# Seven block products for pairs of gate tiles, and output tables made later, in a hybrid attention/SSM block

## The chip, the cores and the metric

The kernel runs on one core of one Trainium2 chip. The metric is the device time of one execution in microseconds (us); a smaller number is better. TensorE (PE) does the matrix products, VectorE (DVE) and ScalarE (ACT) the elementwise work, GpSimd (POOL) a little of it; SyncE (SP) and ACT issue most transfers (DMAs).

## The reference, cut to what matters

```python
h = rms_norm(x)                                   # x: 1024 tokens x 1024
q, k, v, z_a, u, z_s, g_a, g_s = split(h @ W_in)  # 512 wide each, g_a and g_s 1024
y_a = band_attention(q, k, v) * silu(z_a) @ W_attn_out
y_s = GLU(gelu(S5(u))) * silu(z_s) @ W_ssm_out
x = x + (sigmoid(g_a + bias) * y_a + sigmoid(g_s + bias) * y_s) @ W_out
out = rms_norm(x)
```

All in float32. The kernel splits each float32 operand in a high and a low part of the type fp32r, and takes three products: high·high, high·low, low·high.

## The kernel before

`h^T` lies in four tiles: `hT[0]` holds the high parts, `hT[1]` the low parts, each in two tiles `q` = 0, 1 of [128, 4, 1024] (4 of the 8 row tiles of h^T, all 1024 tokens). A *projection* (`proj_task`, with `proj` and `mm3`) takes one 128-row tile of W_in^T, whose raw form `w_raw` is loaded by SP and split into `w_hi` (ACT) and `w_lo` (DVE), and makes two halves of 512 tokens; a half is 8 × 3 = 24 matmuls of 128x512 into one PSUM bank, and an eviction.

The order in time: normalisation and V; projections with the SSM scan beside them; attention, woven into further projections; then, from about 463 us on, the part that the change concerns:

1. The last three g_a tiles (`ga[NGA:]`) and eight g_s tiles (`gs_task`). A g_s eviction is a sigmoid on ACT into a tile `sg`, which SP stores to `sgs_dr` in DRAM.
2. The K=512 stages, through `o_task`: attention output `a_all` (8 tasks), GLU `glu` (8), SSM output `so_all` (8). A task loads a weight tile `o_raw`, splits it (`o_hi`, `o_lo`) and makes two halves of 12 matmuls in three PSUM banks `mm`; between halves it gives way (a "step" of the loops below, numbered n). The moving operands are split before: `split_tiles(za)` for attention output, `split_y_ssm` for GLU, `split_tiles(zs)` for SSM output. `merged` is the sum of both gated branches, kept in `mgd`.
3. W_out. The product of `merged` with W_out is made for pairs of token tiles with seven block products instead of eight (the Winograd form of Strassen's scheme): products P1 to P7 of a left block (A11, A12, A22, S1 to S4) with a right block (B11, B21, B22, T1 to T4), named in `MATES`; `ORDER` names the three banks a, b, c that they add up in. A block product is 4 × 3 = 12 matmuls. `operand` splits a left block.

The right blocks of W_out are 28 *tables* (seven names × four row tiles), each a high and a low part. `make_tables` makes them: for each of four row pairs j it loads two `wo_raw` tiles (in the two slots of `rows`), forms T1 to T4 with four DVE operations, and splits seven results (seven ACT and seven DVE operations). In the kernel before, it runs during the g_s tiles, one step for three k-steps of the projections, through the two slots of `qk_pools[1]` that the last g_a tiles leave; each of the 28 goes to DRAM (`wt_dr`, SP) and comes back by `load_table` (ACT's queue) in the K=512 stages, into the places listed in `SPOTS`.

Memory is given out in pools: a pool has a number of slots for each tag, and a new tile waits until a slot is free. `vp` has eight slots of 4 KB a partition: they hold V during attention, then the high and low parts of the four y tiles of attention output, then those of SSM output. Which instruction comes next on an engine is decided before the run by a planner: it takes, in a simulated time, the ready instruction that the program names first; `tc.high_priority()` puts some ahead, `tc.issue_after` some behind. On the chip each engine then goes through its list in order.

Of the kernel before, what the change touches and what calls it, by code (L numbers as in the profile page):

```python
# [9 lines left out]
F32 = mybir.dt.float32  # L10
F32R = mybir.dt.float32r
# [15 lines left out]
T8 = 8  # L27
# [17 lines left out]
def trunk_kernel(ctx: ExitStack, tc: tile.TileContext, x, x_t, ng, w_m, w_v, bias, a_re, a_im, log_dt,  # L45
# [53 lines left out]
    def split_hi(hi, src):  # L99
        act.activation(out=hi, in_=src, func=AF.Copy)  # L100
# [1010 lines left out]
    def o_task(src, y, evac, before=None, late=False):  # L1111
# [21 lines left out]
        return (o_dma(src), o_split, run, 2)  # L1133

    def gs_task(m):
        def evac(half, ps):
            sg = half_tile()
            act.activation(out=sg, in_=ps, func=AF.Sigmoid, bias=gb[:, KT + m:KT + m + 1])
            nc.sync.dma_start(out=sgs_dr[m][:, cut(half)], in_=sg)
        return proj_task(w_m[28 + m], evac)  # L1140

# [58 lines left out]

    hs, ls = split_tiles(za, vp, "v", "y")
    ya[0].extend(hs)
    ya[1].extend(ls)
    ygr = []

    def load_y(b):
        yr = rows.tile([P, T8, NJ], F32, tag="yr", name="yr")
        nc.sync.dma_start(out=yr, in_=y_dr[b].rearrange("t p j -> p t j"))
        ygr.append(yr)

    wt_dr = {(name, j): dr.tile([P, 2, HALF], F32, name=f"wt_{name}_{j}")
             for name in ("B11", "B21", "B22", "T1", "T2", "T3", "T4") for j in range(4)}

    def make_tables():

        for j in range(4):
# [8 lines left out]
            def keep(name, src):  # L1228
                t = qk_pools[1].tile([P, 2, HALF], F32R, tag="blk", name="wt")
                split_hi(t[:, 0, :], src)  # L1230
                split_lo(t[:, 1, :], src, t[:, 0, :])
                nc.sync.dma_start(out=wt_dr[name, j], in_=t.bitcast(F32))

            def sum_tile():
                return rest.tile([P, HALF], F32, tag="t", name="t", bufs=1)

# [18 lines left out]
    tables = make_tables()  # L1255
    gen = stream.run(ga[NGA:] + [gs_task(m) for m in range(KT)], a_all[:2])
    for _ in range(4 * KT):
        with tc.issue_after(last_turn[0]):
            next(gen)
    for n, _ in enumerate(gen):  # L1260
        if n % 3 == 2:
            next(tables, None)
        if n in (3 * 36 + 4, 3 * 36 + 12):
            load_y((n - 112) // 8)
    wp_cm.__exit__(None, None, None)
    h16_cm.__exit__(None, None, None)
    wo_cm = tc.tile_pool(name="wo", reuse_waits="tile", side="right", bufs=14)
    wo = wo_cm.__enter__()
    mgd.extend(wo.tile([P, 4, L], F32, tag=f"mgd{q}", name="mgd", bufs=1) for q in range(2))

    def split_y_ssm(b):
        v3 = "c (j t) -> c j t"
        src = ygr[b].rearrange("c t j -> c j t")
        hi = wo.tile([P, L], F32R, tag="wb", name="g_hi")
        lo = wo.tile([P, L], F32R, tag="wb", name="g_lo")
        split_hi(hi.rearrange(v3, t=T8), src)
        split_lo(lo.rearrange(v3, t=T8), src, hi.rearrange(v3, t=T8))
        yg[0].append(hi)
# [35 lines left out]

    def operand(src, pool_, tag):
        t = pool_.tile([P, 2, 4, P], F32R, tag=tag, name="a")
        split_hi(t[:, 0], src)
        split_lo(t[:, 1], src, t[:, 0])
        return t

    for n, _ in enumerate(stream.run(so_all)):
        if n > 1 and len(wb) < 28:
            load_table()
        if n == 2 * KT - 2:
            fin_op["A11"] = operand(block(0, "A11"), rows, "yr")
            s3 = rest.tile([P, HALF], F32, tag="t", name="s3", bufs=1).rearrange("p (k m) -> p k m", m=P)
            tt(s3, block(0, "A11"), block(0, "A21"), SUB)
            fin_op["S3"] = operand(s3, rows, "yr")
    assert len(wb) == 28
    rest_cm.__exit__(None, None, None)  # L1330

    ORDER = [("P1", "a", (0,)), ("P2", "b", (0,)), ("P6", "a", (1,)), ("P5", "c", (3,)), ("P7", "a", (3,)),
             ("P3", "c", (1,)), ("P4", "a", (2,))]

# [5 lines left out]
    nc.scalar.dma_start(out=fg_b, in_=fg.partition_broadcast(P))  # L1346
    banks = [(ps_m, "mm")] * 3 + [(ps_2, "s")] * 2 + [(ps_t, "pt")] * 2
    taken = [0]

    def bank():  # L1350
        p_, tag = banks[taken[0] % 7]
        taken[0] += 1
        return p_.tile([P, HALF], F32, tag=tag, name="c")

    for n in range(KT // 2):
# [49 lines left out]
        for pn, bk, to in order:  # L1405
# [13 lines left out]
            for cs in cuts:  # L1419
                for k in range(4):  # L1420
                    w = wb[bn, k]
                    o, h, l = pss[bk][:, cs], w[:, 0, cs], w[:, 1, cs]
                    pe.matmul(o, a[:, 0, k, :], h, start=new and k == 0, stop=False, skip_group_check=True)  # L1423
                    pe.matmul(o, a[:, 0, k, :], l, start=False, stop=False, skip_group_check=True)  # L1424
                    pe.matmul(o, a[:, 1, k, :], h, start=False, stop=k == 3, skip_group_check=True)  # L1425
# [84 lines left out]
```

## Time and profile before

| | us |
|---|---|
| median of 3 runs (lowest, highest) | 800.01 (799.62, 802.39) |
| the profiled execution | 801.95 |
| its span, first to last instruction | 800.2 |
| mean granted clock of TensorE | 0.994 |

The profile is of one execution. A group line reads: source line, engine, operation, output tile <- input tiles, shape, count | busy us, mean ns of one | idle time of the engine before them and who ended it. A line of a tile reads: line, engine, operation, names, count: shortest/median/longest ns, first and last start in us. A line of waits reads: who <- whom: total us, times, longest us.

### The profile page before, as it was taken

How to read it: one execution, taken by the hardware profiler on the slowest of the kernel's cores; microseconds unless marked ns; L12 is line 12 of the kernel's file. 1: busy time of each engine (PE TensorE's matmuls, PEld its weight loads, DVE VectorE, ACT ScalarE, POOL GpSimd, SP SyncE). 2: the span in 40 equal slices, each digit the busy share in tenths (PEclk: the TensorE clock that was granted, in tenths of full speed). 3: DMA queues.
4: the chain of work that ended last, by engine and by line, in shares of the span. 5: the costliest groups of instructions: out<-in, count | busy, mean ns of one | idle time of the engine just before them, and what ended most of it. 6: DMA issues, size and time to landing. Idle time of an engine off the chain costs nothing.

```text
span 800.2 us, 11133 instructions
## 1 busy us (share of the span) xinstructions
PE 786.2 (98%) x3882; PEld 654.3 (82%) x3882; DVE 533.2 (67%) x1382; ACT 371.4 (46%) x670; POOL 115.6 (14%) x162
## 2 busy tenths in 40 slices
PE   8999999999999999999999999999999999999996
PEld 6778888888887888888888888888888888888885
DVE  6899987978746878887555443444163345777874
ACT  5552547546346566666454584434250132122543
POOL 4450021020202233333231100000000000000000
PEclk8999999999999999999999999999999999999999
DMA  8614342423430111110200154898866237722232
GB/s 317 237 28 131 109 91 93 123 57 122 119 138 28 44 44 43 43 43 5 67 27 27 45 196 164 318 331 300 311 212 252 93 106 260 265 65 107 106 117 94
DMA packets 45127, 105.58 MB, mean 132 GB/s; under 512 B 5968, under 2 KB 15184, under 8 KB 45072
## 3 DMA queue, kind: packets, MB, share of 16 engines
q1 hardware_dynamic: 36544, 84.42, 30.5%
q10 hardware_dynamic: 7376, 18.10, 6.6%
q0 software_dynamic: 1152, 2.36, 1.5%
q8 instruction: 30, 0.49, 0.3%
q14 instruction: 25, 0.20, 0.1%
HBM read 75.02 MB, written 29.85 MB: 131 GB/s over the span
## 4 chain that ended last, share of the span: by engine, by line
PE 89%; DVE 6%; ACT 1%; issue 1%; DMA 1%; POOL 0%; DVEq 0%; ACTq 0%
PE mm L108 22%; PE mm L106 22%; PE mm L107 22%; PE c L1423 3%; PE c L1424 3%; PE c L1425 3%; PE pt L957 2%; PE pv L976 2%; PE s L928 1%; PE pv L975 1%; DVE p L930 1%; PE s L929 1%; DVE tl L103 1%; PE pt L456 1%; PE b L482 1%
## 5 line engine op out<-in xcount | busy, mean ns | idle before, releaser
L106 PE MATMUL mm<-hT,w_hi 128*128 128x512 f32 x576 | 233.3, 405 | 0.0
L108 PE MATMUL mm<-hT,w_lo 128*128 128x512 f32 x576 | 226.0, 392 | 0.7 <-DVE w_lo L103 0.7
L107 PE MATMUL mm<-hT,w_hi 128*128 128x512 f32 x576 | 225.4, 391 | 0.0
L108 PEld LDWEIGHTS mm<-hT,w_lo 128*128 128x128 f32 x576 | 108.1, 188 | 24.7 <-DVE w_lo L103 1.1
L107 PEld LDWEIGHTS mm<-hT,w_hi 128*128 128x128 f32 x576 | 108.6, 189 | 16.5 <-issue 0.4
L106 PEld LDWEIGHTS mm<-hT,w_hi 128*128 128x128 f32 x576 | 108.4, 188 | 16.2 <-issue 0.2
L937 ACT ACTIVATE p<-p,mx 128x640 f32<-128x640 f32 (+2 forms) x64 | 44.4, 694 | 33.3 <-DVE mx L89 16.8
L103 DVE TENSOR_TENSOR tl<-pt,th 128x512 fp32r<-128x512 f32 (+2 forms) x72 | 43.0, 600 | 24.5 <-ACT th L100 23.9
L939 POOL TENSOR_SCALAR p<-p,sm 128x640 f32<-128x640 f32 (+2 forms) x64 | 42.5, 666 | 111.5 <-DVE sm L938 80.8
L100 ACT ACTIVATE th<-pt 128x512 fp32r<-128x512 f32 (+2 forms) x72 | 37.6, 523 | 44.6 <-PE pt L957 44.0
L100 ACT ACTIVATE w_hi<-w_raw 128x1024 fp32r<-128x1024 f32 x36 | 38.0, 1055 | 39.3 <-PE mm L107 28.7
L103 DVE TENSOR_TENSOR w_lo<-w_raw,w_hi 128x1024 fp32r<-128x1024 f32 x36 | 44.2, 1229 | 17.2 <-ACT w_hi L100 17.1
L930 DVE CUSTOM_DVE_ANT_0 p<-s,bias 128x320 f32<-128x320 f32 (+2 forms) x96 | 44.2, 485 | 17.2 <-PE s L929 16.7
L106 PE MATMUL mm<-y_hi,o_hi 128*128 128x512 f32 x128 | 49.9, 390 | 0.0
L107 PE MATMUL mm<-y_lo,o_hi 128*128 128x512 f32 x128 | 49.8, 389 | 0.0
L108 PE MATMUL mm<-y_hi,o_lo 128*128 128x512 f32 x128 | 49.8, 390 | 0.0
L100 ACT ACTIVATE o_hi<-o_raw 128x512 fp32r<-128x512 f32 x24 | 15.1, 632 | 70.1 <-PE mm L107 55.5
L1423 PE MATMUL c<-wb,a 128*128 128x512 f32 (+1 forms) x116 | 44.6, 385 | 0.5 <-DVE x L85 0.5
L1424 PE MATMUL c<-wb,a 128*128 128x512 f32 (+1 forms) x116 | 44.7, 385 | 0.0
L1425 PE MATMUL c<-wb,a 128*128 128x512 f32 (+1 forms) x116 | 44.2, 384 | 0.0
L957 PE MATMUL pt<-ident,p 128*128 128x128 f32 x240 | 38.1, 273 | 0.0
L976 PE MATMUL pv<-tl,vt 128*128 128x256 f32 x144 | 36.2, 281 | 1.0 <-DVE tl L103 1.0
(225 smaller groups left out, 1472.3 us busy)
## 6 DMA issues: line engine op xcount, KB each, us to landing
w_raw<-in_w_m_dram SPq DMA_DIRECT2D x36, 512.0 KB, 3.8
x<-in_x_dram SPq DMA_DIRECT2D x16, 512.0 KB, 7.5
wt_T<-wt SPq DMA_DIRECT2D x16, 512.0 KB, 3.4
wb<-wt_T ACTq DMA_DIRECT2D x16, 512.0 KB, 4.9
wt_B<-wt SPq DMA_DIRECT2D x12, 512.0 KB, 4.3
wb<-wt_B ACTq DMA_DIRECT2D x12, 512.0 KB, 5.3
wo_raw<-in_w_out_dram SPq DMA_DIRECT2D x8, 512.0 KB, 6.0
sgs_dr<-sg SPq DMA_DIRECT2D x16, 256.0 KB, 4.6
```

Source lines behind the costliest of these rows:

```text
L100: act.activation(out=hi, in_=src, func=AF.Copy)
L103: (eng or vec).tensor_tensor(out=lo, in0=src, in1=hi.bitcast(F32), op=SUB)
L106: pe.matmul(ps, lh, rh, start=first, stop=False)
L107: pe.matmul(ps, lh, rl, start=False, stop=False)
L108: pe.matmul(ps, ll, rh, start=False, stop=last)
L930: vec.tensor_tensor_reduce(out=pr[:, c * cw:(c + 1) * cw], in0=ps, in1=bt[:, 640 - w + c * cw:640 - w + (c + 1) * cw], scale=1.0, scalar=- ...
L937: act.activation(out=pr[:, :w], in_=pr[:, :w], func=AF.Exp, bias=mx[:, 0:1], accum_out=sm)
L957: last_turn[0] = pe.transpose(tp[:, n:n + P], probs[h, q][:, k * P:(k + 1) * P], ident).ins
L976: pe.matmul(o, lhs, tl[:, cs], start=False, stop=last and n == len(blocks) - 1)
L1423: pe.matmul(o, a[:, 0, k, :], h, start=new and k == 0, stop=False, skip_group_check=True)
L1424: pe.matmul(o, a[:, 0, k, :], l, start=False, stop=False, skip_group_check=True)
L1425: pe.matmul(o, a[:, 1, k, :], h, start=False, stop=k == 3, skip_group_check=True)
```

## The change

- Two g_s tiles (`N1 = 2`) stay projections. The other six run in three pairs (`gs_pairs`): the two weight tiles of a pair, cut in their K halves, are the left blocks, h^T, cut in K halves and token halves, holds the right ones. B11, B21, B22 are parts of `hT` as they lie; T1, T2, T3 are made by `h_sums` on DVE and ACT beside the last g_a tiles and the first two g_s tiles (each h is first added up again from its two parts), and T4 is written over B12 in `hT` once the plain tiles are done (`h_last`). T1 and T2 take the eight slots of `vp`, T3 two of `qk_pools[1]` and two of a new pool `gsp`.
- A block's operand is split from the weight tile (`g_operand`, two blocks ahead, four slots in all); S1 to S4 are four DVE operations a pair. Banks are evicted as partial sums: copies on ACT, additions on DVE, then the sigmoid and the store.
- The y splits of attention output move from before the g_s tiles to the last steps of the pairs, since T1 and T2 hold their slots until then.
- The tables of W_out are made in the K=512 stages: nine steps of `make_tables` from step 7 of attention output on, 24 in GLU, three in SSM output. The first 16 tables are written where W_out reads them; the last twelve go through slots of `vp` to DRAM and come back in SSM output.
- The matmul loop of W_out becomes a function, `block_product`, which the pairs use too.

```diff
+    gsp = gsp_cm.__enter__()
+    half_pool = [gsp, 3]
     def half_tile():
-        return rest.tile([P, HALF], F32, tag="sg", name="sg", bufs=4)
+        return half_pool[0].tile([P, HALF], F32, tag="sg", name="sg", bufs=half_pool[1])
...
-    hs, ls = split_tiles(za, vp, "v", "y")
-    ya[0].extend(hs)
-    ya[1].extend(ls)
+    N1 = 2
+    def block_product(o, a, tab, cs, first):
+        for k in range(4):
+            h, l = tab(k)
+            pe.matmul(o, a[:, 0, k, :], h[:, cs], start=first and k == 0, stop=False, skip_group_check=True)
+            pe.matmul(o, a[:, 0, k, :], l[:, cs], start=False, stop=False, skip_group_check=True)
+            pe.matmul(o, a[:, 1, k, :], h[:, cs], start=False, stop=k == 3, skip_group_check=True)
+    t2s = [vp.tile([P, 2, HALF], F32R, tag="v", name="t2") for _ in range(4)]
+    t1s = [vp.tile([P, 2, HALF], F32R, tag="v", name="t1") for _ in range(4)]
...
+    def h_sums():
+        for r in range(4):
+            b11 = h_sum("o_raw", 0, r, 0, vec)
+            b12 = h_sum("o_lo", 0, r, 1, vec)
+            b22 = h_sum("o_hi", 1, r, 1, vec)
+            yield
+            tt(b22, b22, b12, SUB)
+            tt(b12, b12, b11, SUB)
+            yield
+            tt(b11, b22, b11, ADD)
+            split_tab(h_tab("T3", r), b22)
+            yield
+            split_tab(h_tab("T1", r), b12)
+            yield
+            split_tab(h_tab("T2", r), b11)
+            yield
+        for r in range(4):
+            b21 = h_sum(("o_raw", "o_lo")[r % 2], 1, r, 0, vec)
+            t2 = h_sum2("o_hi", h_tab("T2", r))
+            yield
+            tt(b21, b21, t2, SUB)
+            t4s.append(b21)
+            yield
+    def h_last(r):
+        split_tab(h_tab("T4", r), t4s[r])
...
+    def g_operand(u):
...
+        with tc.high_priority():
+            g_op[u] = operand(src.rearrange("p (k m) -> p k m", m=P), wp, tag)
+        if pn == "P2":
+            g_s1[n] = rest.tile([P, HALF], F32, tag="o_hi", name="s1")
+            a11, a12, a21, a22 = (g_block(b, n) for b in ("A11", "A12", "A21", "A22"))
+            tt(g_s1[n], a21, a22, ADD)
+            tt(a21, a11, a21, SUB)
+            tt(a11, g_s1[n], a11, SUB)
+            tt(a12, a12, a11, SUB)
+    def gs_pairs():
...
+            if u + AHEAD < steps:
+                g_operand(u + AHEAD)
+            if n == 0 and i < 4:
+                h_last(i)
...
+            block_product(ps, g_op.pop(u), lambda k: h_tab(MATES[pn][1], k), slice(0, HALF), new)
+            def done(b, o):
+                m, half = N1 + 2 * n + b // 2, b % 2
+                act.activation(out=o, in_=ps if b == 2 else o, func=AF.Sigmoid, bias=gb[:, KT + m:KT + m + 1])
+                nc.sync.dma_start(out=sgs_dr[m][:, cut(half)], in_=o)
+            if pn in ("P1", "P6", "P5"):
+                b = to[0]
+                out_[b] = half_tile()
+                act.activation(out=out_[b], in_=ps, func=AF.Copy)
+            elif pn == "P4":
+                done(2, half_tile())
+            else:
+                b = to[0]
+                o = out_.pop(b)
+                tt(o, ps, o, ADD)
+                done(b, o)
+            yield
...
+    plain = ga[NGA:] + [gs_task(m) for m in range(N1)]
+    gen = stream.run(plain)
...
+    for u, _ in enumerate(gs_pairs()):
+        if u == n_gs - 8:
+            load_y(0)
+        if u == n_gs - 3:
+            for t in a_all[:2]:
+                stream.load(t)
+        if u == n_gs - 2:
+            load_y(1)
+            hs, ls = split_tiles(za, vp, "v", "y")
+            ya[0].extend(hs)
+            ya[1].extend(ls)
+    stream.split(a_all[0])
...
             def keep(name, src):
-                t = qk_pools[1].tile([P, 2, HALF], F32R, tag="blk", name="wt")
+                if len(wb) < 16:
+                    p_, tag = SPOTS[len(wb)]
+                    t = wb[name, j] = p_.tile([P, 2, HALF], F32R, tag=tag, name="wb")
+                else:
+                    t = vp.tile([P, 2, HALF], F32R, tag="v", name="wt")
                 split_hi(t[:, 0, :], src)
                 split_lo(t[:, 1, :], src, t[:, 0, :])
-                nc.sync.dma_start(out=wt_dr[name, j], in_=t.bitcast(F32))
+                if (name, j) not in wb:
+                    nc.sync.dma_start(out=wt_dr[name, j], in_=t.bitcast(F32))
+                    stored.append((name, j))
...
     tables = make_tables()
-    gen = stream.run(ga[NGA:] + [gs_task(m) for m in range(KT)], a_all[:2])
-    for _ in range(4 * KT):
-        with tc.issue_after(last_turn[0]):
-            next(gen)
-    for n, _ in enumerate(gen):
-        if n % 3 == 2:
-            next(tables, None)
...
     def load_table():
-        name, j = USE[len(wb) // 4], len(wb) % 4
+        name, j = min(stored, key=lambda t: (USE.index(t[0]), t[1]))
+        stored.remove((name, j))
...
     for n, _ in enumerate(stream.run(a_all, glu[:2])):
...
-        if n in (4, 7, 9, 11, 13, 15):
-            load_table()
+        if n >= 7:
+            next(tables)
     for n, _ in enumerate(stream.run(glu, so_all[:2])):
-        if n >= 2 and len(wb) < 16:
-            load_table()
+        for _ in range(1 + (n % 8 not in (0, 1, 6, 7))):
+            next(tables, None)
...
     for n, _ in enumerate(stream.run(so_all)):
-        if n > 1 and len(wb) < 28:
+        next(tables, None)
+        if n > 1 and stored:
             load_table()
```

More of the change, by code (lines that the diff above doesn't have):

```diff
@@ new lines, in trunk_kernel, with bank, operand @@
+    taken = [0]
+    def bank():
+        p_, tag = banks[taken[0] % 7]
+        taken[0] += 1
+        return p_.tile([P, HALF], F32, tag=tag, name="c")
+    def operand(src, pool_, tag):
+        t = pool_.tile([P, 2, 4, P], F32R, tag=tag, name="a")
+        split_hi(t[:, 0], src)
+        split_lo(t[:, 1], src, t[:, 0])
+        return t
+    N1 = 2
[5 more added lines that the diff above has]
+            pe.matmul(o, a[:, 1, k, :], h[:, cs], start=False, stop=k == 3, skip_group_check=True)
@@ new lines, in gs_pairs @@
+    def gs_pairs():
+        AHEAD = 2
+        for u in range(AHEAD):
+            g_operand(u)
+        yield
+        pss, out_ = {}, {}
+        pairs_ = (KT - N1) // 2
+        steps = 7 * pairs_
+        for u in range(steps):
+            n, i = u // 7, u % 7
+            pn, bk, to = ORDER[i]
+            if n < pairs_ - 1 and i in (1, 4):
+                m = N1 + 2 * n + (2 if i == 1 else 3)
+                if m not in g_raw:
+                    g_load(m)
+            if u + AHEAD < steps:
+                g_operand(u + AHEAD)
+            if n == 0 and i < 4:
+                h_last(i)
+            new = (n, bk) not in pss
+            if new:
+                pss[n, bk] = bank()
+            ps = pss[n, bk]
+            block_product(ps, g_op.pop(u), lambda k: h_tab(MATES[pn][1], k), slice(0, HALF), new)
[14 more added lines that the diff above has]
+                done(b, o)
+            yield
@@ L1209, in load_y, with gs_task, evac @@
         ygr.append(yr)
+    def gs_task(m):
+        def evac(half, ps):
+            sg = half_tile()
+            act.activation(out=sg, in_=ps, func=AF.Sigmoid, bias=gb[:, KT + m:KT + m + 1])
+            nc.sync.dma_start(out=sgs_dr[m][:, cut(half)], in_=sg)
+        return proj_task(w_m[28 + m], evac)
+    plain = ga[NGA:] + [gs_task(m) for m in range(N1)]
+    gen = stream.run(plain)
+    sums = h_sums()
+    n_ga = len(plain) * 2 * KT
+    for n in range(n_ga):
+        with tc.issue_after(last_turn[0]) if n < 4 * KT else ExitStack():
+            next(gen)
+        if n % 2 == 1:
+            next(sums, None)
+        if n == 40:
+            g_load(N1)
+            g_load(N1 + 1)
@@ new lines, in trunk_kernel @@
+    for _ in sums:
+        pass
+    for _ in gen:
+        pass
+    g_load(N1 + 2)
+    n_gs = 7 * (KT - N1) // 2
+    for u, _ in enumerate(gs_pairs()):
[10 more added lines that the diff above has]
+    stream.split(a_all[0])
+    gsp_cm.__exit__(None, None, None)
@@ new lines, in trunk_kernel, with split_y_ssm @@
+    late_cm = tc.tile_pool(name="late", reuse_waits="tile", bufs=2)
+    late = late_cm.__enter__()
+    half_pool[:] = [late, 4]
+    wp_cm.__exit__(None, None, None)
+    h16_cm.__exit__(None, None, None)
+    wo_cm = tc.tile_pool(name="wo", reuse_waits="tile", side="right", bufs=14)
+    wo = wo_cm.__enter__()
+    mgd.extend(wo.tile([P, 4, L], F32, tag=f"mgd{q}", name="mgd", bufs=1) for q in range(2))
+    def split_y_ssm(b):
+        v3 = "c (j t) -> c j t"
+        src = ygr[b].rearrange("c t j -> c j t")
+        hi = wo.tile([P, L], F32R, tag="wb", name="g_hi")
+        lo = wo.tile([P, L], F32R, tag="wb", name="g_lo")
+        split_hi(hi.rearrange(v3, t=T8), src)
+        split_lo(lo.rearrange(v3, t=T8), src, hi.rearrange(v3, t=T8))
+        yg[0].append(hi)
+        yg[1].append(lo)
@@ L1214, in trunk_kernel @@
+    SPOTS = [(wo, "wb")] * 6 + [(qk_pools[n // 5], "blk") for n in range(10)] + [(wo, "wb")] * 8 + [(zp, "z")] * 4
+    wb = {}
+    USE = ["B11", "T3", "B21", "T2", "T1", "B22", "T4"]
     wt_dr = {(name, j): dr.tile([P, 2, HALF], F32, name=f"wt_{name}_{j}")
              for name in ("B11", "B21", "B22", "T1", "T2", "T3", "T4") for j in range(4)}
+    stored = []
     def make_tables():
@@ L1325, in trunk_kernel @@
             fin_op["A11"] = operand(block(0, "A11"), rows, "yr")
[L1326 removed]
+            s3 = late.tile([P, HALF], F32, tag="t", name="s3", bufs=1).rearrange("p (k m) -> p k m", m=P)
             tt(s3, block(0, "A11"), block(0, "A21"), SUB)
@@ L1419, in trunk_kernel @@
             for cs in cuts:
[L1420 to L1425, printed above, removed]
+                block_product(pss[bk][:, cs], a, lambda k: (wb[bn, k][:, 0, :], wb[bn, k][:, 1, :]), cs, new)
                 for b in to:
```

86 lines of the change are left out of this document (45 added, 41 removed).

## The prediction

> **What bounds the kernel now.** I read the page first, the granted clock with it, then the stretches by stage, then what TensorE (PE) waited for.
>
> ```profile
> span 800.2 us, 11133 instructions
> PE 786.2 (98%) x3882; PEld 654.3 (82%) x3882; DVE 533.2 (67%) x1382; ACT 371.4 (46%) x670; POOL 115.6 (14%) x162
> PEclk8999999999999999999999999999999999999999
> PE 89%; DVE 6%; ACT 1%; issue 1%; DMA 1%; POOL 0%; DVEq 0%; ACTq 0%
> ```
>
> PE is busy for 98% and makes 89% of the chain that ended last. Busy time alone does not say that PE is at its best, so the stretches come next: the first two are the K=1024 projections, then attention output, GLU, SSM output and W_out (x is the number of instructions; DMA share and GB/s stand last).
>
> ```profile
> core 0: us, PE busy (x) PEld busy (x) DVE busy (x) ACT busy (x) POOL busy (x), PEclk, DMA share, GB/s
> 463.00:517.00 54.00, 54.00 (x244) 44.78 (x243) 21.84 (x28) 30.96 (x47) 1.29 (x1) 1.00 0.67 236
> 517.00:582.60 65.60, 65.60 (x291) 54.34 (x290) 24.22 (x32) 23.26 (x35) 0.00 (x0) 1.00 0.82 297
> 582.60:626.50 43.90, 43.90 (x194) 35.95 (x193) 22.13 (x26) 13.02 (x12) 0.00 (x0) 1.00 0.67 228
> 626.50:671.30 44.80, 44.80 (x193) 35.91 (x193) 19.43 (x27) 13.59 (x20) 0.00 (x0) 1.00 0.36 112
> 671.30:714.80 43.50, 43.50 (x193) 35.99 (x193) 29.65 (x46) 6.85 (x11) 0.00 (x0) 1.00 0.61 217
> 714.80:796.30 81.50, 78.16 (x350) 63.64 (x348) 62.19 (x140) 34.33 (x76) 0.00 (x0) 1.00 0.28 103
> ```
>
> From 463 us on PE has no hole until W_out's tail, at the full clock, and neither DVE nor ACT passes 77%. So in this region a matmul taken away is time taken away, and anything that makes PE wait is time added. The price of a matmul is its start-to-start distance, not its recorded 390 ns (records overlap):
>
> ```profile
> L1138 ACT ACTIVATE sg<-mm,gb x16: 665/672/693, 501.3 to 582.9; 128x512 f32<-128x512 f32 x16
> L107 PE MATMUL mm<-g_lo,o_hi x64: 394/394/394, 626.8 to 670.9; 128*128 128x512 f32 x64
> L1423 PE MATMUL c<-wb,a x102: 388/394/398, 714.9 to 784.8; 128*128 128x512 f32 x102
> ```
>
> The g_s evictions follow each half of 24 matmuls: 81.6 us over 15 × 24 gives 226.7 ns. GLU: 44.1 us over 63 × 3 gives 233.3 ns. W_out up to 785 us: 69.9 us over 101 × 3 gives 230.7 ns. The same instruction thus has two paces, 226.7 and 233.3; W_out, whose blocks have the shape of the new ones, mixes them.
>
> **The change, part by part.** *Matmuls.* Six tiles of 48 matmuls become three pairs of seven products of 12: 288 become 252. Removed: 36 × 226.7 ns = 8.16 us. The 252 that stay move to block products; at W_out's 230.7 ns they cost 252 × 4.0 ns = 1.01 us more. Ends: 226.7 costs nothing, 233.3 costs 1.66 us. I take W_out's, the same code.
>
> The trace has 226.7 to 233.3 ns in every stage here. The Trainium skill ("TensorE: Matmul & The Clock Gate", Back-to-back issue gap) gives about 131 ns for each N=512 matmul in a stream with weight loads; by that 36 matmuls would bring 4.7 us instead of 8.16. No stage of this trace comes near 131 ns, so the trace decides.
>
> *Will the blocks be fed?* Durations:
>
> ```profile
> L100 ACT ACTIVATE a<-s 128x512 fp32r<-128x512 f32 x16 | 10.0, 628 | 19.6 <-DVE s L85 11.6 <-PE c L1425 7.9
> L103 DVE TENSOR_TENSOR a<-s,a 128x512 fp32r<-128x512 f32 x16 | 10.8, 685 | 1.3 <-ACT a L100 1.1
> L85 DVE TENSOR_TENSOR x<-c,x 128x512 f32<-128x512 f32 x29 | 19.7, 687 | 11.0 <-PE c L1425 7.5 <-DMA x<-in_x_dram 3.3
> PE c L1423 <- DVE x L85: 0.5, 1, 0.5
> ```
>
> A pair lasts 84 × 0.2307 = 19.4 us. DVE has seven operand splits (0.685), three bank additions and four weight sums (0.69): 9.6 us. ACT has seven splits (0.63), three copies and four sigmoids (0.67): 9.1 us. Both hide, at half of PE's time. A bank is written again one block (2.7 us) after its eviction may begin, and the eviction takes 0.69; four operand slots allow preparation up to three blocks ahead. W_out with the same order and fewer operand slots cost PE one wait of 0.5 us in 28 blocks. I take 0; ends 0 and 21/28 of 0.5, say 0.4 us.
>
> *Sums of h^T.* DVE: 4 × (6 sums + 3 low parts), 4 × 3 for T4's source, 4 low parts of T4: 52 × 0.69 = 35.9 us; ACT 16 × 0.63 = 10.1 us. T2 is due at the third block, 240 × 0.2267 + 5.4 = 60 us after the last attention products near 463. DVE's 21.8 us in the first stretch lose the tables' share (11 us or so, from the 30 below spread over 96 us, and the later y splits) and gain 33: about 41 of 54 us. Hidden; were that cover gone, each late sum of four rows would hold PE up by 4 × 0.69 = 2.8 us. The tile loads (six of 512 KB) move within SP's queue; the 28 table stores leave this stretch, so those loads run with less beside them. Cost 0.
>
> *Attention's y splits move* from 452–476 us to the last four blocks:
>
> ```profile
> L100 ACT ACTIVATE y_hi<-z x4: 1051/1060/1061, 451.6 to 474.7; 128x1024 fp32r<-128x1024 f32 x4
> L103 DVE TENSOR_TENSOR y_lo<-z,y_hi x4: 1224/1224/1227, 456.6 to 475.8; 128x1024 fp32r<-128x1024 f32 x4
> ```
>
> They take T2's and T1's slots, free 10.9 and 8.2 us before the attention-output stage. DVE then has 4 × 1.22, two bank additions, three operand splits and o_lo: 9.0 us; ACT 4 × 1.06, four evictions, three splits: 8.8 us. It just fits in 10.9, and only y's k=0 is due at once, k=3 two us later. I take 0.3 us; ends 0 and 1.5 (one y split behind the rest).
>
> *Tables of W_out.* Four sets, each 11 DVE operations (7.6 us) and 7 ACT splits (4.4 us), move into the K=512 stages: DVE rises there from 50% to about 65%. Stores fall from 28 to 12 on SP, loads from 28 to 12 on ACT's queue; SP's remaining stores now stand among the o_raw and sg loads, which are issued a task (5.4 us) early. None of that is on PE's path unless something waits, and two things can:
>
> ```profile
> DVE t L85 <- DMA wo_raw<-in_w_out_dram: 8.4, 3, 6.4
> L100 ACT ACTIVATE wt<-wo_raw x20: 617/632/635, 491.6 to 569.0; 128x512 fp32r<-128x512 f32 x20
> L103 DVE TENSOR_TENSOR g_lo<-yr,g_hi x4: 2011/2030/2041, 585.6 to 596.4; 128x1024 fp32r<-128x1024 f32 x4
> wt_B<-wt SPq DMA_DIRECT2D x12, 512.0 KB, 4.3
> wb<-wt_B ACTq DMA_DIRECT2D x12, 512.0 KB, 5.3
> wo_raw<-in_w_out_dram SPq DMA_DIRECT2D x8, 512.0 KB, 6.0
> ```
>
> First, DVE waited up to 6.4 us for a w_out row tile. Before, only a weight's low part stood behind it, once in 10.9 us. Now a stage's evictions do. With three banks an eviction may be 2 × 2.72 − 0.69 − 0.3 = 4.4 us late; 6.4 would cost 2.0 us, the other two waits (1.0 mean) nothing.
>
> Second, the SSM-output stage's own operands. The last y split ended just in time:
>
> ```profile
> 671.84 0.74 DVE L94 SCALAR_TENSOR_TENSOR sg<-mm,bg,sg 128x512 f32<-128x512 f32 x1
> 672.50 0.68 DVE L103 TENSOR_TENSOR o_lo<-o_raw,o_hi 128x512 fp32r<-128x512 f32 x1
> 673.10 0.68 DVE L85 TENSOR_TENSOR zs<-zs,sg 128x512 f32<-128x512 f32 x1
> 674.48 0.69 DVE L103 TENSOR_TENSOR y_lo<-zs,y_hi 128x512 fp32r<-128x512 f32 x1 [0.70 <-ACT y_hi L100]
> 675.46 0.39 PE L106 MATMUL mm<-y_hi,o_hi 128*128 128x512 f32 x1
> ```
>
> That low part ends at 675.17 and PE's matmul with it starts at 675.69: 0.5 us to spare. One table operation of 0.69 us in that chain on DVE costs 0.2 us, two cost 0.9. I take 0.6.
>
> **The sum** in the profiled execution (span 800.2, time 801.95, so 1.75 around it): −8.16 + 1.01 + 0.3 + 0.6 = −6.25, a span of 794.0 and a time of 795.7. That execution stands 1.94 above the median of 800.01, to which I put the same difference: 793.8 us.
>
> **The rivals.** *A, the last tables find no room.* The twelve stored tables pass through vp's eight slots, which y of SSM output fills. y's pairs were made here:
>
> ```profile
> L100 ACT ACTIVATE y_hi<-zs x5: 632/1059/1059, 640.0 to 673.8; 128x1024 fp32r<-128x1024 f32 x3, 128x512 fp32r<-128x512 f32 x2
> ```
>
> In the new clock (7 us earlier): three pairs by 655, the fourth at 666. Row tiles need `rows` slots, free after the last g_lo at 598.4 − 7 = 591; plus 6 to land. A set takes 7.6 us of the 57 to 68% of DVE that is free, 11 to 13, plus about 6 to land the next: starts at 597, 613, 630, 649; the last set runs from 649 to 663. From 655 on it has two slots. Two slots gave 28 tables in 78 us before, 2.8 us a table: three done by 655, four more by 666, just when the fourth y takes the last two. A table left over waits for SSM output's last matmuls: slot free 2.7 us before the end, then 0.63 + 0.69 + 0.4 + 4.3 + 0.4 + 5.3 = 11.7 us, and W_out's first product wants B11's fourth part 2.1 us in: a stall of 6.9 us, giving 793.8 + 6.9 = 800.7, slower than before. It decides if B11 of the last set is left over; if only B22 or T4 are, which are wanted 13.7 us or more later, it costs nothing. For it: the tie. Against: B11 needs no sum and can be made as soon as its row lands.
>
> *B, small waits in the K=512 stages*: a 6.4 us wait for a row tile twice (4.0 us), or y's last pair waiting for a table's store (up to 4.3 − 0.5 = 3.8 us): 797.8 us. The Trainium skill (the same page, Architectural detail) has VectorE and ScalarE as strict FIFO, so an eviction cannot pass a table operation that waits. The ordered rows of this trace agree: in the fence above o_lo stood between the two GLU steps and zs followed it. For B: DVE up to 65%. Against: 12 stores instead of 28.
>
> *C, pace only.* A stage keeps the pace that it falls into: attention and SSM output (192 matmuls each) at 233.3 instead of 226.7 would cost 1.3 us each, GLU at 226.7 would save 1.3. With the blocks at 233.3: 793.8 + 0.65 + 2.6 = 797.0; all at the fast pace: 793.8 − 1.0 − 1.3 − 0.9 (no stalls) = 790.6.
>
> *D, the blocks starve*: DVE or ACT order holds each of the 21 blocks up by the 0.69 of one operation: 14.5 us, 808 us. Only W_out's single wait bears on it, and speaks against.
>
> **How the numbers follow.** 0.5% (4 us: 796.0 and 804.0) is what a measurement of this kernel can tell from no change. Forecast with C's fast end (790.6 to 796): 0.56. B and C's slow end (796 to 798): 0.21. A (796 to 803 by how much is left over): 0.15, of which 0.03 above 804. D: 0.08. Faster 0.56; same 0.21 + 0.12 = 0.33; slower 0.11. The range runs from C's fast end to A's 800.7, rounded up for a store slower than its median: 790.5 to 801.5; the forecast's own is 790.6 to 796.
>
> **What would show it.** Right: 3846 matmuls; seven products in about 19.4 us, three times; attention output begins near 575 us; PE without idle up to W_out; 28 tables, 12 stored, the last store before 670. Wrong: a PE wait at the first product of W_out behind a wb load (A), PE waits for mm banks or y_lo in the K=512 stages (B), the start distances at 233 ns (C), PE waits behind DVE or ACT within the pairs (D).

## The result, and the profile after

The changed kernel is slower: median 812.02 us (810.29 to 813.93, 4 runs) against 800.02 us (799.62 to 802.39, 4 runs) of the kernel before, ratio 1.0144 [1.0113, 1.0176]. The forecast was 793.8 us, the range 790.5 to 801.5. The profiled execution took 811.26 us. The lines of its page that the prediction began with:

```profile
span 809.5 us, 11096 instructions
PE 783.0 (97%) x3846; PEld 647.5 (80%) x3846; DVE 582.2 (72%) x1470; ACT 390.8 (48%) x710; POOL 117.7 (15%) x162
PEclk9999999999999999999999999999999999978998
PE 81%; DVE 9%; DMA 4%; issue 2%; ACT 2%; ACTq 0%; POOL 0%; DVEq 0%
```

The 36 matmuls are gone (3882 to 3846). But PE's share of the chain that ended last falls from 89% to 81%, and a slice near the end has a clock of 0.7. The stretches are, in order: plain projections, pairs (with the first 24 matmuls of attention output among them), attention output, GLU, SSM output, and W_out in three parts:

```profile
core 0: us, PE busy (x) PEld busy (x) DVE busy (x) ACT busy (x) POOL busy (x), PEclk, DMA share, GB/s
463.00:515.30 52.30, 52.30 (x234) 43.34 (x233) 42.02 (x63) 31.09 (x50) 1.80 (x1) 1.00 0.24 83
515.30:578.50 63.20, 63.20 (x278) 51.88 (x277) 30.67 (x43) 29.99 (x47) 0.00 (x0) 1.00 0.40 136
578.50:620.40 41.90, 39.69 (x169) 30.91 (x169) 33.64 (x46) 20.39 (x25) 0.00 (x0) 1.00 0.40 128
620.40:665.40 45.00, 45.00 (x194) 35.70 (x193) 31.84 (x48) 19.78 (x31) 0.00 (x0) 1.00 0.66 228
665.40:709.30 43.90, 43.79 (x194) 35.91 (x192) 28.71 (x45) 7.39 (x13) 0.00 (x0) 1.00 0.36 120
709.30:722.00 12.70, 9.18 (x33) 6.16 (x33) 5.25 (x9) 1.01 (x2) 0.00 (x0) 0.91 1.01 384
722.00:733.50 11.50, 4.82 (x12) 3.44 (x11) 4.28 (x7) 3.23 (x6) 0.00 (x0) 0.50 0.99 396
733.50:804.00 70.50, 68.29 (x306) 55.56 (x304) 53.93 (x124) 29.85 (x69) 0.00 (x0) 1.00 0.21 76
```

The pairs have no hole in PE. Attention output has some. In W_out, PE does 12 matmuls in the 11.5 us behind 722, at half clock, while the DMA engines are full. The next table has the lengths of the stages in us, with three of the experiments below beside them; a stage ends where the next one's unbroken run of matmuls begins. (In e1, e5 and e10 three, one and two matmuls of W_out, 0.2 us each, stand earlier, among SSM output's, and are counted there.) Between executions the part ahead of these stages differs by up to 2.7 us, between equal programs too (it ends at 465.6 us in e1's trace and at 463.5 in e2's, and they are the same there), so stages are compared by their lengths and not by their times of day:

| | before | after | e1 | e5 | e10 |
|---|---|---|---|---|---|
| plain projections, pairs, attention output | 160.64 | 156.88 | 157.47 | 157.25 | 155.97 |
| GLU | 44.80 | 44.96 | 45.54 | 45.40 | 44.80 |
| SSM output | 43.54 | 44.24 | 44.26 | 43.79 | 44.03 |
| W_out, to its last matmul | 78.30 | 92.30 | 77.81 | 78.31 | 78.06 |
| sum | 327.28 | 338.38 | 325.08 | 324.75 | 322.85 |

W_out alone lost 14.0 us. PE's waits and ACT's longest name the place:

```profile
PE c L1227 <- ACT a L100: 7.8, 3, 6.7
PE mm L106 <- DVE mgd L85: 1.6, 3, 1.0
PE c L1227 <- DMA wb<-wt_B: 1.5, 2, 1.0
PE c L1227 <- DMA wb<-wt_T: 0.9, 1, 0.9
```

```profile
ACT a L100 <- DMA wb<-wt_T: 17.0, 1, 17.0
```

PE waits for tables (2.4 us), but most for an operand split that ACT owes it, and ACT stood still for 17.0 us at loads of tables. The stored tables' splits and stores, by tile, and then ACT's timeline behind 706 us (start, length):

```profile
L100 ACT ACTIVATE wt<-wo_raw x9: 615/617/636, 628.3 to 708.0; 128x512 fp32r<-128x512 f32 x9
L1467 SPq DMA_DIRECT2D wt_B<-wt x6: 319/320/1177, 630.3 to 710.4; - x6
```

```profile
706.97 1.68 ACT L100 ACTIVATE wt<-wo_raw 128x512 fp32r<-128x512 f32 x3 [8.21 <-PE mm L107]
708.54 1.13 ACT L100 ACTIVATE a<-mgd 128x512 fp32r<-128x512 f32 x2
711.20 0.33 ACTq L1498 DMA_DIRECT2D wb<-wt_B  x1
711.56 1.19 ACTq L1498 DMA_DIRECT2D wb<-wt_T  x1
712.79 0.98 ACTq L1498 DMA_DIRECT2D wb<-wt_B  x2
713.82 2.32 ACTq L1498 DMA_DIRECT2D wb<-wt_T  x3
718.90 0.33 ACTq L1498 DMA_DIRECT2D wb<-wt_B  x1
723.22 4.17 ACTq L1498 DMA_DIRECT2D wb<-wt_T  x2
727.98 1.67 ACT L100 ACTIVATE a<-s 128x512 fp32r<-128x512 f32 x3 [16.98 <-DMA wb<-wt_T]
```

Three tables (B11, B21 and B22 of j = 3) were split only at 707, when SSM output's last matmuls let go of `vp`'s slots (`<-PE mm L107`). The first load in ACT's list is that of the late B11: it could leave only when its store had landed, at 711.2. Nine more loads, seven of them of tables that had been stored between 629 and 651, stood behind it, and the splits `a<-s` behind those. Between 717 and 721 PE waited three times for a table, 0.6 to 1.0 us each; it was at half clock from 720.8 on and stood still from 722 to 729.

### The profile page after: what moved, and what is told of

The parts are those of the page before. It is cut to its first block, busy times and chain, and to the rows that moved or that the text cites. A ratio compares the mean times of both kernels' runs of the same rounds, so it can differ in the third digit from the quotient of the medians.

```text
span 809.5 us, 11096 instructions
## 1 busy us (share of the span) xinstructions
PE 783.0 (97%) x3846; PEld 647.5 (80%) x3846; DVE 582.2 (72%) x1470; ACT 390.8 (48%) x710; POOL 117.7 (15%) x162
## 4 chain that ended last, share of the span: by engine, by line
PE 81%; DVE 9%; DMA 4%; issue 2%; ACT 2%; ACTq 0%; POOL 0%; DVEq 0%
PE mm L106 18%; PE mm L108 18%; PE mm L107 17%; PE c L1227 5%; PE c L1228 5%; PE c L1229 5%; PE pt L957 2%; DMA wb<-wt_T 2%; PE pv L976 2%; PE s L928 1%; PE pv L975 1%; DVE p L930 1%; PE s L929 1%; DVE tl L103 1%; DMA wo_raw<-in_w_out_dram 1%
## 5 line engine op out<-in xcount | busy, mean ns | idle before, releaser
L106 PE MATMUL mm<-hT,w_hi 128*128 128x512 f32 x480 | 196.0, 409 | 0.0
L108 PE MATMUL mm<-hT,w_lo 128*128 128x512 f32 x480 | 188.7, 393 | 0.7 <-DVE w_lo L103 0.7
L107 PE MATMUL mm<-hT,w_hi 128*128 128x512 f32 x480 | 188.1, 392 | 0.0
L108 PEld LDWEIGHTS mm<-hT,w_lo 128*128 128x128 f32 x480 | 90.1, 188 | 21.0 <-DVE w_lo L103 1.1
L107 PEld LDWEIGHTS mm<-hT,w_hi 128*128 128x128 f32 x480 | 90.6, 189 | 12.8 <-issue 0.4
L106 PEld LDWEIGHTS mm<-hT,w_hi 128*128 128x128 f32 x480 | 90.4, 188 | 12.4 <-issue 0.2
L937 ACT ACTIVATE p<-p,mx 128x640 f32<-128x640 f32 (+2 forms) x64 | 44.4, 694 | 33.3 <-DVE mx L89 16.4
L1227 PE MATMUL c<-wb,a 128*128 128x512 f32 (+1 forms) x116 | 46.3, 402 | 10.8 <-ACT a L100 7.8
L100 ACT ACTIVATE w_hi<-w_raw 128x1024 fp32r<-128x1024 f32 x30 | 31.7, 1058 | 44.1 <-PE mm L107 33.6
L107 PE MATMUL mm<-y_lo,o_hi 128*128 128x512 f32 x128 | 49.9, 389 | 0.0
L103 DVE TENSOR_TENSOR w_lo<-w_raw,w_hi 128x1024 fp32r<-128x1024 f32 x30 | 37.0, 1232 | 14.9 <-ACT w_hi L100 14.8
L1228 PE MATMUL c<-wb,a 128*128 128x512 f32 (+1 forms) x116 | 45.7, 394 | 0.0
L1229 PE MATMUL c<-wb,a 128*128 128x512 f32 (+1 forms) x116 | 44.2, 393 | 0.0
L1227 PEld LDWEIGHTS c<-wb,a 128*128 128x128 f32 x116 | 22.4, 193 | 18.7 <-ACT a L100 9.4
```

Of the source, the lines that this page charges most:

```text
L103: (eng or vec).tensor_tensor(out=lo, in0=src, in1=hi.bitcast(F32), op=SUB)
L106: pe.matmul(ps, lh, rh, start=first, stop=False)
L107: pe.matmul(ps, lh, rl, start=False, stop=False)
L108: pe.matmul(ps, ll, rh, start=False, stop=last)
L937: act.activation(out=pr[:, :w], in_=pr[:, :w], func=AF.Exp, bias=mx[:, 0:1], accum_out=sm)
L1227: pe.matmul(o, a[:, 0, k, :], h[:, cs], start=first and k == 0, stop=False, skip_group_check=True)
```

## The experiments

The ratios of e1 to e4 are against 800.91 us of the kernel before, measured beside them (22 runs).

**e1: the last three tables straight to their places** (no `vp` slot, no store, no load).

```diff
-                if len(wb) < 16:
+                if len(wb) < 16 or (j == 3 and name in ("B11", "B21", "B22")):
```

> The changed kernel, with the last three tables (B11, B21, B22 of the fourth row pair) written straight into the places where W_out reads them, free since GLU's end, instead of through vp and DRAM. Theory (slots of vp are given in the program's order, so these three wait behind the eight y tiles until SSM output is over, and their loads hold ACT's queue): no PE wait and no cold clock in W_out, which again takes about 78.5 us from its first to its last matmul instead of 92.3; 812.0 - 13.8 = 798 us (797 to 799.5). Rival (W_out is late because so many table loads fall into it or because DVE and ACT are behind): W_out keeps waits of 5 us or more, 805 us or above.

798.48 us (796.51 to 799.87, 10 runs), ratio 0.9968 [0.9953, 0.9982]. W_out takes 77.81 us: all 14 us come back, and the changed kernel without this one fault is a little faster than before.

**e2: the loads of the tables that are ready go first in ACT's list**, those of the three late ones last; the three are as late as in the changed kernel.

```diff
-        name, j = min(stored, key=lambda t: (USE.index(t[0]), t[1]))
+        late_ = [(b, 3) for b in ("B11", "B21", "B22")]
+        name, j = min(stored, key=lambda t: (t in late_, USE.index(t[0]), t[1]))
```

> The changed kernel, with only the order of the twelve loads changed: the three late tables are loaded last. The three are still made after SSM output's last matmuls. Theory: nine loads then run during SSM output, three stay late; PE waits once for B11's fourth part, some 4 to 6 us at the start of W_out, and ACT's queue is not held, so no 6.7 us wait for an operand split; 803 to 806 us. If the lateness of the three alone made the loss (rival), the time stays at 811 to 813. If the late making is harmless and only the queue order counts: 798.

800.43 us (797.58 to 802.51, 10 runs), ratio 0.9989 [0.9973, 1.0004]. Nearer to the last rival (798) than to my theory (803 to 806): late tables are cheap (PE waits 1.6 us for one, W_out takes 81.5 us), nine loads and the operand splits behind a late one are not.

**e3 and e4: the tables alone.** No pairs and no sums of h^T (`N1 = KT`, y splits where they were), tables in the K=512 stages as in the changed kernel; e4 has e1's line besides.

> All eight g_s tiles as plain projections again (no block products, no sums of h), the y splits of attention output at their old place, but W_out's tables made in the K=512 stages as in the changed kernel. Theory: the late tables cost the same 14 us here and DVE's load in attention output another 1 to 3: 815 to 819 us. Rival (the pairs make the loss, by what they displace): 800 to 804.

> As the one before (no pairs, tables in the K=512 stages), with the last three tables written straight into W_out's places. Theory: what is left is the waits in attention output behind table operations on DVE, 1 to 3.5 us: 801 to 803.5 us; against the run with pairs and direct tables this is 4 to 7 us more, which is what the block products bring. If the pairs bring nothing, both are equal.

e3: 817.61 us (816.15 to 818.89, 4 runs), ratio 1.0207 [1.0182, 1.0232], as expected. e4: 805.48 us (803.48 to 805.94, 7 runs), ratio 1.005 [1.0032, 1.0067], slower than expected. So the late three cost 12.1 us here, the pairs bring 805.48 − 798.48 = 7.0 us, and the moved tables cost some 4 us even without the late three. In e4's trace 2.6 us of these lie in attention output (46.4 us, before 43.8). The stretch, and PE's waits in it:

```profile
582.50:628.90 46.40, 44.74 (x194) 35.59 (x193) 34.66 (x48) 21.33 (x27) 0.00 (x0) 1.00 0.40 131
```

```profile
PE mm L108 <- DVE o_lo L103: 0.9, 2, 0.5
PE mm L106 <- DVE mgd L85: 0.8, 1, 0.8
```

DVE is busy there for 34.7 us, where before it was for 22.1, and what PE waits for (o_lo, the eviction mgd) is DVE's. Behind the longest gap stands a late row of w_out: DVE did nothing for 1.42 us, with the eviction two operations further on in its list.

```profile
601.70 0.69 DVE L85 TENSOR_TENSOR wo_raw<-wo_raw 128x512 f32<-128x512 f32 x1 [1.42 <-DMA wo_raw<-in_w_out_dram]
602.31 0.68 DVE L103 TENSOR_TENSOR wb<-t,wb 128x512 fp32r<-128x512 f32 x1
602.91 0.68 DVE L85 TENSOR_TENSOR mgd<-mm,mg 128x512 f32<-128x512 f32 x1
603.65 0.50 PE L106 MATMUL mm<-y_hi,o_hi 128*128 128x512 f32 x1 [0.75 <-DVE mgd L85]
```

This matmul starts 1.14 us after the one before it, where 0.23 is the usual distance, so 0.91 us were lost. The other two gaps are waits for o_lo: 0.66 us lost at 600.3, with a split g_lo and one operation of the tables ahead of it, and 0.56 at 618.5, with a run of the tables' operations ahead of it that had begun, at 612.9, behind another such stop of 1.50 us.

**e5: the tables ahead of y in the program.** Nothing but the order in which slots are asked for is changed.

```diff
+    for _ in tables:
+        pass
     hs, ls = split_tiles(zs, vp, "v", "y", (3,))
```

> One thing moved in the changed kernel (812.0 us): the generator of the tables is run to its end ahead of the eight y tiles in the program, so that the last three tables take their slots of vp before y does; their twelve stored tables, the places of the loads in the order of the program and everything else stay. Theory (slots of one tag are given out in the program's order, so y's eight tiles, named first, kept the last three tables waiting until SSM output let them go at 707): the three are split in the GLU stage, all twelve loads leave during SSM output, W_out has no stop and takes 78 us: 798 to 800 us. Rival (vp has no room at that time, whatever the order, so y is then late instead): SSM output starts late by some us, 803 us or more. Rival (a tie of timing, as the prediction had it): the order in the program changes nothing, 811 to 813 us.

797.23 us (795.99 to 798.98, 6 runs) against 799.68 of before, measured beside it (13 runs, which e6 to e8 share), ratio 0.9971 [0.9959, 0.9982]. The tiles `wt` in its trace:

```profile
L100 ACT ACTIVATE wt<-wo_raw x9: 615/617/634, 631.1 to 650.1; 128x512 fp32r<-128x512 f32 x9
L1467 SPq DMA_DIRECT2D wt_B<-wt x6: 319/476/1196, 633.1 to 652.8; - x6
```

The last table is split at 650, not 708, and the time is a little under the 798 to 800 of the theory, which stands. Slots of a tag go out in the program's order; it was no race. The changed kernel's trace says the same: the rest of the last set was split by 650.2 and the rows of these three had landed by 643.2, and yet it was y that got the slots, with splits as late as 656.6, 664.4 and 667.7.

**e6: the loads from GpSimd's queue**, the three tables late as in the changed kernel.

```diff
-        nc.scalar.dma_start(out=t.bitcast(F32), in_=wt_dr[name, j])
+        nc.gpsimd.dma_start(out=t.bitcast(F32), in_=wt_dr[name, j])
```

> The changed kernel (812.0 us) with the twelve loads of tables issued from GpSimd's queue instead of ScalarE's; the last three tables are still split at 707 and stored at 709, and ten loads still leave after 711. Theory (most of the price was ScalarE's queue, on which the splits of W_out's operands stood behind loads that could not be issued): the operands come when they are due, PE waits only for tables that land late, from 712 to about 717 for B11 and some us behind it: 802 to 806 us. Rival (the transfers themselves are too late, ten of them and the x rows at 384 GB/s): 809 to 812 us. Second rival (the order of the queue is all that counts, as the run with the ready loads first suggests): 799 to 801 us.

803.32 us (802.22 to 804.59, 4 runs), ratio 1.0049 [1.0032, 1.0066], as the theory expected. GpSimd now stands in ACT's place, at no cost; its first and last loads in W_out, and PE's longest wait:

```profile
712.61 0.53 POOL L1498 DMA_DIRECT2D wb<-wt_B  x1 [47.56 <-DMA wt_B<-wt]
723.82 0.53 POOL L1498 DMA_DIRECT2D wb<-wt_T  x1 [3.05 <-DMA wb<-wt_T]
```

```profile
PE c L1227 <- DMA wb<-wt_B: 2.0, 1, 2.0
```

W_out takes 82.4 us. So of its 14.0 us, 9.9 were ACT's list held up (with the half clock that came of it), and 4.1 the tables' own lateness.

**e7 and e8: no step of the tables in attention output's loop.** e7: two steps for each of GLU's and the last four in SSM output; e8: GLU keeps 24, SSM output takes 12. Tables made in SSM output go straight to the places that GLU has left.

```diff
-        if n >= 7:
-            next(tables)
...
-                if len(wb) < 16:
+                if len(wb) < 16 or in_ssm[0]:
```

> No step of the tables in the attention-output stage: two for each step of GLU (32 of 36) and the last four in SSM output, where the tables go straight to the places that GLU has left, so eight are stored and loaded, not twelve. Theory (what the moved tables cost besides the late three, 805.5 against 800.9 us without pairs, is VectorE's FIFO in the attention-output stage, whose evictions and o_lo splits stand behind the tables' operations): of PE's 3 to 5 us of waits in that stage the one at its start (1.1 us, mgd behind hT) stays, the others go, and VectorE at some 35 of 45 us in GLU gives less than 1 us of new ones: 795 to 797 us. Rival (the same operations give the same waits wherever they stand): 798 to 800 us.

> As the run before it, but GLU keeps its 24 steps and SSM output takes the other 12, its ten or eleven tables straight to their places, so one or two are stored. Theory (VectorE's load in a stage makes the waits): attention output loses its waits as there; SSM output, where VectorE was busy for 29 of 43 us, goes to some 38 to 40 of 43 and gets waits of 2 to 4 us of its own: 797 to 800 us. Rival (the stage does not matter, and what is saved is the stores and loads): 795 to 797 us.

e7: 796.99 us (796.57 to 797.78, 5 runs), ratio 0.9967 [0.9954, 0.998]. e8: 797.38 us (796.47 to 798.02, 7 runs), ratio 0.9972 [0.9961, 0.9983]. Both times lie in the ranges of their theories (795 to 797, 797 to 800), but by luck: they are e5's time, and the mechanism did not come about. Attention output in e7 is what it was in the changed kernel.

```profile
578.00:619.80 41.80, 39.78 (x170) 30.92 (x169) 33.61 (x46) 20.40 (x25) 0.00 (x0) 1.00 0.40 129
```

DVE has 33.61 us there still, in 46 instructions. The loop in which a step stands does not hold it: the planner takes each operation as early as it can start. In e8 it has 33.72. So these two runs say nothing on attention output's waits. In e8's SSM output DVE is busy for 35.1 of 44.4 us, and PE waits once, for 0.6 us, not for 2 to 4.

**e10: e8 with the tables held** behind attention output's last eviction; one step, which only loads rows, stands free ahead of GLU.

```diff
-            tt(merged(m, cut(half)), ps, ga_, MUL)
+            last_ao[0] = vec.tensor_tensor(out=merged(m, cut(half)), in0=ps, in1=ga_, op=MUL).ins
...
-            next(tables, None)
+            with tc.issue_after(last_ao[0]):
+                next(tables, None)
```

> The kernel with no step of the tables in the attention-output stage's loop kept them there all the same: the planner took the tables' operations as soon as they could start. Here they are held by an order behind attention output's last eviction, 24 steps in GLU's loop and 12 in SSM output's. Theory (VectorE's load where it stands): attention output has the wait at its start alone, some 2 to 2.5 us less, but VectorE has then some 40 of 45 us in GLU and 37 of 43 us in SSM output, and waits come there, 1 to 3 us: 0.995 to 0.998 of before. Rival (only the attention-output stage is tender, for its two evictions and one split follow each other within 5.4 us there too, but its y and g splits of 2.0 us stand in the same FIFO): 0.993 to 0.994.

794.78 us (794.51 to 795.81, 4 runs) against 800.18 (9 runs, shared with e9, e11 and e12), ratio 0.993 [0.9915, 0.9946]: faster than both kernels. Attention output, GLU, SSM output, and PE's waits in these stages:

```profile
578.40:619.50 41.10, 38.81 (x170) 31.33 (x169) 21.42 (x25) 13.04 (x12) 0.00 (x0) 1.00 0.33 105
619.50:664.30 44.80, 44.80 (x194) 35.91 (x193) 39.31 (x60) 24.79 (x40) 0.00 (x0) 1.00 0.47 154
664.30:708.30 44.00, 44.00 (x196) 36.38 (x195) 35.11 (x57) 10.71 (x19) 0.00 (x0) 1.00 0.45 160
```

```profile
PE mm L106 <- DVE mgd L1151: 2.3, 2, 1.3
```

DVE is back to 21.4 us in attention output, and o_lo's waits are gone. With 39.3 of 44.8 us in GLU and 35.1 of 44.0 in SSM output PE has no wait in either: my theory (a full DVE makes waits wherever it is) falls, the rival (attention output alone is tender) holds. The wait of 1.3 us that is left is none of the tables': the eviction stands behind g_lo, a split of GLU's operands, as the rival had said.

```profile
594.92 1.99 DVE L103 TENSOR_TENSOR g_lo<-yr,g_hi 128x1024 fp32r<-128x1024 f32 x1 [0.97 <-ACT g_hi L100]
596.82 0.69 DVE L1151 TENSOR_TENSOR mgd<-mm,mg 128x512 f32<-128x512 f32 x1
597.66 0.47 PE L106 MATMUL mm<-y_hi,o_hi 128*128 128x512 f32 x1 [1.33 <-DVE mgd L1151]
```

Against e5 the medians' ratios give 3.3 us; the traces place 1.3 us in attention output and 0.6 in GLU; the rest has no place in a stage, and the intervals of the two ratios leave room for that.

**e9, e11, e12: the tables' 28 low parts on GpSimd**, in e5, in e8 and in e4.

```diff
-                split_lo(t[:, 1, :], src, t[:, 0, :])
+                split_lo(t[:, 1, :], src, t[:, 0, :], pool)
```

> The kernel with the tables ahead of y in the program (0.997 of before), with the 28 subtractions that make the tables' low parts on GpSimd instead of VectorE (its row before: 128x512 to fp32r in 1.57 us, so 44 us over three stages in which it was idle). Theory (VectorE's FIFO makes the waits of PE in the attention-output stage): VectorE loses some 12 operations of 0.69 us there, the waits behind mgd and o_lo at 596 to 618 us and at 629 go, 2 to 2.5 us of them; the one at the start of the stage (1.1 us) stays: 0.994 of before, 795 us where before takes 800. Rival (the waits are not VectorE's load but ScalarE's or the loads of rows): no change against the kernel it starts from, 0.997. Rival on the other side (GpSimd and VectorE slow each other, tables come late): 0.999 or more.

> The kernel with 12 steps of the tables in SSM output (0.997 of before), with the 28 low parts on GpSimd. Theory (VectorE's load): as in the run on GpSimd above, and SSM output's one wait behind o_lo (1.0 us) goes too: 0.993 to 0.994 of before. Rival (GpSimd's 1.57 us each makes the last tables late for W_out's first blocks): a wait of PE for a table at W_out's start, 0.997 or more.

> The kernel without pairs and sums of h^T, its tables in the K=512 stages and the last three straight to their places (1.005 of before), with the 28 low parts on GpSimd. Theory (the cost of moving the tables, besides the late three, is VectorE's load in the attention-output stage, where PE waited 2.6 us): that stage takes 43.6 to 44.2 us again, not 46.2, and the time is 1.001 to 1.002 of before. Rival (the cost is elsewhere, in W_out or at the end): 1.004 to 1.006 still.

All three are slower than the kernels they start from, and no theory holds. e9 805.93 us (804.78 to 808.73, 4 runs), ratio 1.0072 [1.0046, 1.0099]; e11 805.57 (802.57 to 806.27, 6 runs), 1.0055 [1.0037, 1.0073]; e12 809.28 (808.76 to 811.41, 4 runs), 1.0117 [1.0094, 1.014]. e9 is where its second rival had it (0.999 or more); e11 has its rival's time without its mechanism, for PE waits for no table in W_out; e12 is beyond its rival too. e9's DVE, GpSimd and PE, in one place:

```profile
613.35 0.68 DVE L85 TENSOR_TENSOR mgd<-mm,mg 128x512 f32<-128x512 f32 x1
616.37 1.76 DVE L103 TENSOR_TENSOR o_lo<-o_raw,o_hi 128x512 fp32r<-128x512 f32 x1
618.05 1.76 DVE L85 TENSOR_TENSOR t<-wo_raw 128x512 f32<-128x512 f32 x1
619.73 0.68 DVE L85 TENSOR_TENSOR mgd<-mm,mg 128x512 f32<-128x512 f32 x1
613.35 1.31 POOL L103 TENSOR_TENSOR wb<-wo_raw,wb 128x512 fp32r<-128x512 f32 x1 [2.21 <-ACT wb L100]
616.31 4.64 POOL L103 TENSOR_TENSOR wb<-wo_raw,wb 128x512 fp32r<-128x512 f32 x3 [0.41 <-ACT wb L100]
618.18 0.62 PE L108 MATMUL mm<-y_hi,o_lo 128*128 128x512 f32 x1 [2.43 <-DVE o_lo L103]
618.60 0.63 PE L106 MATMUL mm<-y_hi,o_hi 128*128 128x512 f32 x1
```

Beside GpSimd's operations DVE's o_lo and t take 1.76 us here, not 0.69, and PE waits 2.43 us for o_lo (DVE had also stood still for 1.68 us before 615.71, for a late w_out row). The eviction mgd beside it keeps its 0.68. The Trainium skill ("SBUF — State Buffer", Who interferes with whom) has the rule: a DVE instruction with two inputs in SBUF contends with a GpSimd instruction that reads SBUF, one with at most one such input, outside the 2-port modes, does not. The trace agrees on both kinds: o_lo and t read two SBUF tiles, mgd one and a PSUM bank. So these runs took no load off DVE (33.2 us in e9's attention output, 33.7 in e5's), and e12 does not tell where e4's cost lies; e10 does, for the part in attention output.

## Why the prediction was wrong

*Matmuls: right.* 36 left, and the pairs without the late tables bring 7.0 us (e4 against e1) where the sum had 8.16 − 1.01 − 0.3 = 6.85. The pace term was near: 276 matmuls from 515.4 to 578.55 make 228.7 ns, with 24 plain ones at 226.7 among them, so 228.9 for the blocks: 252 × 2.2 ns = 0.55 us instead of 1.01.

*Blocks fed, sums of h^T hidden: right.* PE is busy for 63.20 of 63.20 us in the pairs, DVE for 42.0 of 52.3 in the stretch for which 41 of 54 was worked out. Rival D had nothing to it.

*y splits: the price near, another mechanism.* They made no wait in the pairs. The planner put attention output's first 24 matmuls in among the last blocks instead; their banks were then full, and the evictions could not write until a gate's last store:

```profile
581.70 1.89 DVE L85 TENSOR_TENSOR mgd<-mm,mg 128x512 f32<-128x512 f32 x3 [4.54 <-DMA sgs_dr<-sg]
582.45 0.50 PE L106 MATMUL mm<-y_hi,o_hi 128*128 128x512 f32 x1 [0.97 <-DVE mgd L85]
```

The start distance there is 1.36 us, so 1.1 us lost, within the 0 to 1.5 of the term. That `mgd` lies over the memory of those tiles is my reading; no run moved it.

*Tables, 0.6 us: the step that was too small where it was looked at, and the one that failed where it was dismissed.* First, the term looked at two waits (a w_out row late, SSM output's start), took 0.6 for the second and nothing for the first, nor for the tables' operations that stand between attention output's evictions and splits. Its figure for DVE's load was low as well: the prediction's own rows give 71.2 us before plus 30.4 for four sets, in 132.2 us, so 77% and not 65%; the trace after has 94.2 of 130.8, 72%. Holding the operations back (e10) made that stage 1.3 us and GLU 0.6 us shorter. e4's ratio puts the whole at 4.0 us (2.6 to 5.4 by its interval); its trace has 2.6 of them in attention output, 0.2 in GLU and 0.25 in W_out. Another 0.7 stands behind W_out's last matmul, in a stretch that differs by up to 1.0 us between the runs. This is rival B, small waits behind DVE's strict order, near its price of 4.0: B had a row late by 6.4 us twice, and what came were rows late by 1.4 and 1.5 us with a list of table operations behind them, so that rows and the operations' number share the loss. No run parts the two. Second, SSM output's start, where the 0.6 was put, cost nothing: GLU and SSM output together took 89.20 us against 88.34, and 0.7 us of this is a wait for W_out's first operand, ACT having split the late tables ahead of it.

*Rival A was what happened, and the step that failed is its condition and its price.* The place was right: no room in `vp`, so a stop in W_out. "It decides if B11 of the last set is left over" was called a tie of timing, 666 against 666, and given 0.15. There was no tie: `vp`'s slots go out in the order in which the program names the tiles, y's eight stand ahead of the last three tables, and they waited for them whatever DVE could do (e5). The rest of their set was done by 650, 16 us before the 666 at which the tie was put. The planner's choice is among ready instructions, not among slots. The price, 6.9 us for B11's own way through DRAM, was 14.0: B11's lateness is in the 4.1 us that stay when the loads leave ACT's queue, and the other 9.9 are the nine loads and the operand splits that stood behind its load in ACT's list (e2, e6). The working costed the late tile and did not ask what is queued behind the instruction that waits for it. "The last store before 670" was the mark to see it by: it left at 710.4.

With both repaired (e10) the change gives −5.4 us, against −6.25 forecast; 2.3 us of PE's waits for mgd remain, 1.0 behind the gate's store and 1.3 behind g_lo.

## What to carry to other kernels

Before moving buffers' makers later, list the requests for each slot in the program's order: a tile named behind others waits for all of them, even when it is ready and they are not. For each transfer that can be late, read what else is in its issuing engine's list: a late load should stand last, or on an engine that owes nobody work. Where a planner orders instructions, a step's place in the source does not hold it back; only a stated order does.

## What the hardware showed that I had not expected

- GpSimd does not take elementwise work off DVE for nothing: with it, DVE's operations on two SBUF tiles took up to 1.76 us instead of 0.69, and the kernel lost 1.0% (e9 against e5).
- A load that cannot leave yet holds up its issuing engine's computing: ACT made nothing for 17.0 us. With transfers of 512 KB under way its last loads left only at 718.90, 723.22 and 727.07, each 0.02 us after an earlier transfer had landed (718.88, 723.20, 727.05). The records of the trace give the reason: each of the three waits for the semaphore (108, 110, 102) that this earlier transfer signals, and takes it over. ACT's and SP's transfers share eight semaphores in this program, all eight were in use, and in none of the traces does a transfer leave before the earlier one on its semaphore has landed. GpSimd's queue has eight others; in e6 eight loads left at once and the ninth at 720.24, after the first had landed (719.72). So the eight is the program's number; a limit of the queues themselves no run here shows.
- TensorE's clock halves after short stops. In e9 the matmuls behind the wait of 2.43 us were recorded with 0.62 us and started every 0.43 us until 621.6, 3.4 us later (granted clock 0.53). Two waits of 1.40 and 1.45 us close together did the same in e12 (0.57 from 619.7 to 623.7), and in the changed kernel three of 0.59, 0.95 and 0.96 us within 4 us (0.50 from 720.8 on). A single wait of 1.95 us in e6 did not (1.00). So it is not the length of one stop alone that decides. The Trainium skill ("TensorE: Matmul & The Clock Gate", What's actually happening) gives an idle window of about 3.4 us for this; all these stops were shorter, so the measurement decides: a wait of 2.4 us, or several shorter ones, can already cost the clock.
